# An MLP's two products on one core: residual by accumulating DMAs, gated fetches, two pairs stored late, weight loads in turn

## The chip, the cores and the metric

The kernel runs on one core of a Trainium2 chip. The metric is the device time of one execution in microseconds (us); of the kernel before it is the median of three runs, 2515.09 us (2513.76 to 2515.51). A core has TensorE (PE, with its weight loads as PEld), VectorE (DVE), ScalarE (ACT), GpSimd (POOL) and SyncE (SP). DMAs are issued here from SP and from POOL.

## The reference

One layer of a hybrid trunk on x of 512 x 2048 in float32: two branches (attention and a gated unit), merged and added to x, and then an MLP with a hidden width of 8192. The change touches the MLP alone:

```python
    x = x + merged @ w_out[l]
    h2 = rms_norm(x, g_ff[l])
    x = x + jnp.square(jax.nn.relu(h2 @ w_ff1[l])) @ w_ff2[l]
```

The `x` in front of the last `+` is called the residual below.

## The kernel before

**A product of float32.** Every operand is split into two parts, `hi` (cast on ACT, L107) and `lo` (the rest, by a subtraction on DVE, L108), and `mm3` (L70 to L74) issues three matmuls: hi x hi (L72), hi x lo (L73), lo x hi (L74). A weight thus goes from DRAM to a tile `w_raw`, through ACT to `w_hi`, through DVE to `w_lo`, and then to PE.

**Strassen's form.** Both MLP products use a scheme of seven products with sums of the four blocks of each operand. `NAMES` gives the seven names: y11, y21, m7, m6, y22, m4, m5. The class `Sums` (L161 to L190) loads the four weight blocks w11, w12, w21, w22 in its constructor (L169 and L170, each a DMA of 512 KB on SP), and makes the sums when a product is due: a = w11 + w21 on DVE for m7 (L176), an accumulating DMA on POOL that adds w22 to w21 (L178, where `loaded` is true; otherwise an addition on DVE for m5, L184), c = a + w22 for m6 (L180), c + w12 for y22 (L182). Six tiles per object: four blocks, a and c.

**The first product.** `hidden(p)` (L796) computes 256 hidden columns, a pair of 128, with `strassen_columns` (L192); there are 32 pairs, two of them computed plainly. The results of a pair (`act`, two tiles) are squared and made into the seven left operands of the second product, stored in DRAM as `store[f]`, f = p // 4. `keep_hidden` (L696) does it in steps that stand in the list `behind` and are called by `step()` while the following pair is computed. Pair 31, the last, goes through `keeping` (L732), seven steps of 256 KB each in chunk 1.

**The second product.** It goes over 8 chunks f of 1024 hidden columns, and in each over two halves g of 1024 output columns: `strassen_tokens` (L220). A half runs seven products; each has two row groups i, two token tiles t and two row blocks k, so 8 turns of `mm3` or 24 matmuls. Row group i = 0 takes its six weight tiles from the pool `raw`, i = 1 from the pool `more`, which is opened (L854) on the memory of the pool `long` when that is closed (L853). `long` holds twelve tiles that the first product reads: y11 of 8 blocks, and y21 of four (L686). The left operands come back from `store[f]` by `fetch(f, name)` (L813): four DMAs of 256 KB on POOL into tiles `ys` of the pool `slots`.

**The residual.** x after the branches lies in DRAM as `kept`. 16 tiles `x2` of 128 x 512 are loaded from it by `residual` (L837 to L840, 256 KB each on POOL), and `evac_y` (L866) adds each product's result to them on DVE (L869). In the last chunk the tiles go to the output.

**What orders the work.** The engines run their queues in order; a scheduler arranges the instructions by their dependences. `between(name)` (L875) is called behind each product and issues fetches; in chunk 0 it also issues residual loads. A DMA on SP or POOL waits, besides its data and its buffer, for the DMA eight places earlier on the same queue. `tc.issue_after` makes the instructions inside it depend on a given one. The last call of `hidden` and the first of `strassen_tokens` follow each other with no barrier.

Of the kernel before, what the change touches and what calls it, by code (L numbers as in the profile page):

```python
# [16 lines left out]
P = 128  # L17
# [18 lines left out]
def tile_hybrid_layer(ctx: ExitStack, tc: tile.TileContext, x, g_mix, w_in, g_q, g_k, ln_g, ln_b,  # L36
# [124 lines left out]
    class Sums:  # L161


        def __init__(self, blocks, tiles, loaded=True):


            self.blocks, self.loaded = blocks, loaded
            self.w11, self.w12, self.w21, self.w22, self.a, self.c = tiles
            for t, hc in ((self.w11, (0, 0)), (self.w12, (1, 0)), (self.w21, (0, 1)), (self.w22, (1, 1))):  # L169
                state["load"] = nc.sync.dma_start(out=t, in_=blocks[hc])  # L170
            self.take = {"y11": self.w11, "y21": self.w12, "m7": self.a, "m6": self.c, "y22": self.w12,
                         "m4": self.w22, "m5": self.w21}

        def parts(self, name):
# [17 lines left out]
    def strassen_columns(wap, c0, rhs, forks, evac, loaded=True):  # L192
# [4 lines left out]
        w = Sums(blocks, [state["raw"].tile([P, KH, P], F32, name="w_raw", tag="w_raw") for _ in range(6)],  # L197
                 loaded)
        trunk, side = acc("q"), acc("q")
        for name in TREE:  # L200
# [18 lines left out]

    def strassen_tokens(wap, r0, c0, lhs, evac, between, loaded=True, after=None):  # L220

        KQ = 2
        ws = []
        for i in range(2):
            rows = wap[r0 + i * 2 * KQ * P:r0 + (i + 1) * 2 * KQ * P, :]
            blocks = {(h, c): rows[:, c0 + c * W:c0 + (c + 1) * W].rearrange("(k h p) c -> h p k c", p=P, h=2)[h]
                      for h in range(2) for c in range(2)}
            pool = (state["raw"], state["more"])[i]
            ws.append(Sums(blocks, [pool.tile([P, KQ, W], F32, name="w_raw", tag="w_raw") for _ in range(6)],
                           loaded))  # L230
        banks = {}
        for name in NAMES:
            b, new = BANK[name]
            if new:
                banks[b] = [(aux if b in (1, 3) else acc)("q") for _ in range(2)]
            for i in range(2):
                with tc.issue_after(after.ins) if after and name == "m7" else nullcontext():
                    hi, lo = ws[i].parts(name)
                for t in range(2):
                    for k in range(KQ):  # L240
                        y = [part[:, t * P:(t + 1) * P] for part in lhs[name][i * KQ + k]]
                        mm3(banks[b][t], y, (hi[:, k, :], lo[:, k, :]), new and i == 0 and k == 0,
                            i == 1 and k == KQ - 1, skip_group_check=True)
            for t in range(2):
                evac(name, t, banks[b][t])
            between(name)
            step()
# [411 lines left out]

    def factor(ys, act, k, name, scale=None):  # L660


        y11, y12, y21, y22 = act[0][:, :HS], act[0][:, HS:], act[1][:, :HS], act[1][:, HS:]
        o, in0, in1, op = {"m7": (y22, y12, y22, ALU.subtract), "m6": (y22, y22, y11, ALU.subtract),
                           "m4": (y22, y21, y22, ALU.add), "m5": (y12, y11, y12, ALU.subtract)}[name]
        nc.vector.tensor_tensor(out=o, in0=in0, in1=in1, op=op)
        ys[name, k] = halves(o, scale=scale)

# [11 lines left out]
    for b in range(KT):  # L680
# [3 lines left out]
        for half in range(2):  # L684
            name = "y" + "12"[b % 2] + "12"[half]
            far = name == "y11" or name == "y21" and b // 2 < LONG - KT // 2  # L686
            hs[name, b // 2] = halves(y[:, half * HS:(half + 1) * HS], long if far else slots)
# [64 lines left out]
    for p in range(PLAIN):  # L752
        o = [acc("f1") for _ in range(2)]
        for kt in range(0, KT, 4):
            hi, lo = weight(w_ff1[0], kt, p * 2 * P, 2 * P)
            if p == PLAIN - 1:
                for i in range(kt, kt + 4):
                    factor(hs, x2T[i % 8 * 2:i % 8 * 2 + 2], i % 8, "m7" if i < 8 else "m6",
                           -1.0 if i < 8 else None)
            for c in range(2):  # L760
# [66 lines left out]
    pairs = DFF // (2 * P)  # L827
    for p in range(PLAIN, pairs - 1):
        acts.append(hidden(p))
# [3 lines left out]
        behind.extend([lambda fs=fs: [f() for f in fs if f] for fs in zip_longest(*ready)])  # L833
    act = hidden(pairs - 1)
    flush()

    def residual(half, t, c):  # L837
        tb, j = 2 * half + t, c
        x2[tb, j] = slot("x2")
        nc.gpsimd.dma_start(out=x2[tb, j], in_=kept[tb, j])  # L840

    lhs = {}

    def fetch_first(name):
        lhs[name] = fetch(0, name)
        if name in ("y11", "m7", "m6", "y22"):
            half, c = {"y11": (0, 0), "m7": (1, 1), "m6": (0, 1), "y22": (1, 0)}[name]
            for t in range(2):
                residual(half, t, c)

    for name in NAMES[:3]:
        fetch_first(name)
    first.close()  # L853
# [5 lines left out]
             "m5": [(1, 1, ALU.subtract), (1, 0, ALU.add)]}  # L859
    done = {"y21": [(0, 0)], "m4": [(0, 1)], "m5": [(1, 1), (1, 0)]}  # L860
    for f in range(chunks):
        ahead = {}
        if f == 1:
            behind.extend(keeping(pairs - 1, act))
        for g in range(2):
            def evac_y(name, t, o):  # L866
                for half, c, op in takes[name]:
                    a = x2[2 * half + t, 2 * g + c]
                    nc.vector.tensor_tensor(out=a, in0=a, in1=o, op=op)  # L869
                if f == chunks - 1:  # L870
                    for half, c in done.get(name, []):
                        tb, j = 2 * half + t, 2 * g + c
                        nc.sync.dma_start(out=out[tb * P:(tb + 1) * P, j * W:(j + 1) * W], in_=x2[tb, j])

            def between(name):  # L875
# [3 lines left out]
                if f == 0:  # L879
                    if g == 0 and i + 3 < len(NAMES):  # L880
                        fetch_first(NAMES[i + 3])
                    for half, c in {(0, "m4"): [(0, 2)], (1, "y11"): [(1, 3)], (1, "y21"): [(0, 3)],
                                    (1, "m7"): [(1, 2)]}.get((g, name), []):
                        for t in range(2):
                            residual(half, t, c)
                    i = i - 6 if g == 0 else i + 1
                    asked = 0 <= i < len(NAMES)
                else:
                    i += g * 5
                    asked = i < (5 if g == 0 else 7)  # L890
                if f < chunks - 1 and asked:
                    ahead[NAMES[i]] = fetch(f + 1, NAMES[i])

            strassen_tokens(w_ff2[0], f * GROUP * 2 * P, g * 2 * W, lhs, evac_y, between,
                            loaded=f > 0, after=None if f or g else state["evac"])
        lhs = ahead
# [25 lines left out]
```

## Time and profile before

| | |
|---|---|
| median of three runs | 2515.09 us |
| the profiled execution, its own time | 2515.18 us |
| its span in the profile | 2513.1 us |
| granted clock of PE, mean | 0.994 |
| PE busy | 2474.6 us (98%) |
| DVE busy | 1617.4 us (64%) |
| ACT busy | 1068.7 us (43%) |
| POOL busy | 329.4 us (13%) |
| DRAM traffic | 346.58 MB read, 67.11 MB written |

The time is the slowest core's whole execution; the span is from the first to the last recorded instruction, here 2.1 us less. Busy time is given by engine; the brackets behind an instruction give the idle time ahead of it and what ended it, so `[8.00 <-ACT w_hi L107]` is 8 us of waiting that ended with ACT's cast of line 107. `q` and `fork` are accumulators of PE, `ys` the left operands. The DMA share is the mean busy share of the 16 DMA engines. `SPq` and `POOLq` are the DMA queues of SP and POOL. The second product's first matmul starts at 1873.41 us in the span.

### The profile page before, as it was taken

What the parts mean: (1) busy time and instruction counts of PE and PEld (TensorE: products, weight loads), DVE (VectorE), ACT (ScalarE), POOL (GpSimd) and SP (SyncE); (2) the same over time, 40 slices, a digit from 0 to 9 for tenths busy, and PEclk for the clock granted to TensorE, in tenths of its full rate; (3) what the DMA queues carried; (4) which work ended last, traced back from release to release, by engine and by line L of the source; (5) the groups of instructions that cost most, each with busy time, mean ns of one, the idle gap of its engine ahead of it and who ended that gap; (6) DMA issues with size and microseconds to landing.
All of it is one profiled execution on the core that took longest, in us unless ns stands there. A gap on an engine that the chain in (4) does not pass through costs nothing.

```text
span 2513.1 us, 32248 instructions
## 1 busy us (share of the span) xinstructions
PE 2474.6 (98%) x12221; PEld 2092.2 (83%) x12221; DVE 1617.4 (64%) x2078; ACT 1068.7 (43%) x1507; POOL 329.4 (13%) x420
## 2 busy tenths in 40 slices
PE   8999999999999999999999999999988999999999
PEld 7888888888888888888888888888876888888887
DVE  4555463223335343322689888888878989889887
ACT  5233342122322322232467776777753443333333
POOL 0212110000121010100000000000023223212210
PEclk9999999999999999999999999999998999999999
DMA  5322222333333233344259888888887887767763
GB/s 176 92 84 76 92 68 92 94 100 97 114 100 101 93 100 118 118 149 136 85 141 266 217 225 230 221 230 234 216 293 288 260 280 243 229 219 215 250 180 96
DMA packets 346381, 415.82 MB, mean 165 GB/s; under 512 B 16961, under 2 KB 224369, under 8 KB 346225
## 3 DMA queue, kind: packets, MB, share of 16 engines
q1 hardware_dynamic: 289248, 320.94, 39.6%
q0 software_dynamic: 56976, 92.82, 15.5%
q8 instruction: 96, 1.57, 0.3%
q14 instruction: 61, 0.49, 0.1%
HBM read 346.58 MB, written 67.11 MB: 165 GB/s over the span
## 4 chain that ended last, share of the span: by engine, by line
PE 95%; DMA 2%; DVE 2%; ACT 1%; issue 0%; SPq 0%; POOL 0%; DVEq 0%; ACTq 0%; POOLq 0%
PE q L73 10%; PE q L72 10%; PE q L74 10%; PE q L209 7%; PE fork L209 7%; PE q L211 3%; PE fork L211 3%; PE xo L74 2%; PE xo L72 2%; PE xo L73 2%; PE gb L72 2%; PE gb L73 2%; PE gb L74 2%; PE ga L72 2%; PE ga L73 2%; PE ga L74 2%
## 5 line engine op out<-in xcount | busy, mean ns | idle before, releaser
L107 ACT CAST w_hi<-w_raw 128x1024 fp32r<-128x1024 f32 x434 | 456.8, 1052 | 558.6 <-PE q L73 357.0
L96 DVE TENSOR_TENSOR w_lo<-w_raw,w_hi 128x1024 fp32r<-128x1024 f32 x216 | 268.1, 1241 | 595.7 <-ACT w_hi L94 591.6
L108 DVE TENSOR_TENSOR w_lo<-w_raw,w_hi 128x1024 fp32r<-128x1024 f32 x434 | 530.7, 1224 | 142.9 <-ACT w_hi L107 142.1
L94 ACT CAST w_hi<-w_raw 128x1024 fp32r<-128x1024 f32 x216 | 227.2, 1052 | 664.7 <-PE ga L73 99.6
L73 PE MATMUL q<-w_lo,ys 128*128 128x512 f32 x896 | 351.8, 393 | 9.5 <-DVE w_lo L108 9.5
L74 PE MATMUL q<-w_hi,ys 128*128 128x512 f32 x896 | 350.8, 392 | 0.0
L72 PE MATMUL q<-w_hi,ys 128*128 128x512 f32 x896 | 316.8, 393 | 8.0 <-ACT w_hi L107 8.0
L209 PE MATMUL q<-ys,w_hi 128*128 128x512 f32 x720 | 260.9, 400 | 4.2 <-ACT fork L215 3.5
L209 PE MATMUL fork<-ys,w_hi 128*128 128x512 f32 x720 | 258.4, 399 | 0.3 <-ACT fork L215 0.3
L73 PEld LDWEIGHTS q<-w_lo,ys 128*128 128x128 f32 x896 | 169.6, 189 | 47.2 <-DVE w_lo L108 12.1
L72 PEld LDWEIGHTS q<-w_hi,ys 128*128 128x128 f32 x896 | 169.6, 189 | 43.9 <-ACT w_hi L107 8.4
L211 PE MATMUL q<-ys,w_lo 128*128 128x256 f32 x720 | 203.1, 282 | 0.0
L211 PE MATMUL fork<-ys,w_lo 128*128 128x256 f32 x720 | 202.5, 281 | 0.0
L74 PEld LDWEIGHTS q<-w_hi,ys 128*128 128x128 f32 x896 | 169.5, 189 | 35.2
L178 POOL DMA_DIRECT2D w_raw<-in_w_ff_dram x57 | 79.4, 1393 | 772.9 <-ACT relu L803 399.9
L869 DVE TENSOR_TENSOR x<-x,q 128x512 f32<-128x512 f32 x256 | 168.2, 683 | 5.7 <-PE q L74 4.1
L209 PEld LDWEIGHTS q<-ys,w_hi 128*128 128x128 f32 x720 | 136.2, 189 | 35.7 <-ACT fork L215 4.1
L209 PEld LDWEIGHTS fork<-ys,w_hi 128*128 128x128 f32 x720 | 135.5, 188 | 32.3 <-ACT fork L215 0.6
L818 POOL DMA_DIRECT2D ys<-store x224 | 124.6, 568 | 251.9 <-PE q L74 180.4
L211 PEld LDWEIGHTS q<-ys,w_lo 128*128 128x128 f32 x720 | 137.2, 190 | 1.2
L211 PEld LDWEIGHTS fork<-ys,w_lo 128*128 128x128 f32 x720 | 136.3, 189 | 1.2
L72 PE MATMUL xo<-w_hi,mT_hi 128*128 128x512 f32 x256 | 100.6, 393 | 0.0
(277 smaller groups left out, 4843.4 us busy)
## 6 DMA issues: line engine op xcount, KB each, us to landing
w_raw<-in_w_ff_dram SPq DMA_DIRECT2D x256, 512.0 KB, 5.4
w_raw<-in_w_in_dram SPq DMA_DIRECT2D x144, 512.0 KB, 3.5
ys<-store POOLq DMA_DIRECT2D x224, 256.0 KB, 6.0
w_raw<-in_w_ff_dram POOLq DMA_DIRECT2D x57, 512.0 KB, 6.8
store<-ys_hi SPq DMA_DIRECT2D x93, 256.0 KB, 4.8
store<-ys_lo SPq DMA_DIRECT2D x93, 256.0 KB, 5.5
w_raw<-in_w_out_dram SPq DMA_DIRECT2D x32, 512.0 KB, 3.7
store<-ys SPq DMA_DIRECT2D x38, 256.0 KB, 5.7
```

The costliest lines, as they stand in the source:

```text
L72: nc.tensor.matmul(o, lhsT=lh[0], rhs=rh[0], start=start, stop=False, **kw)
L73: nc.tensor.matmul(o, lhsT=lh[0], rhs=rh[1], start=False, stop=False, **kw)
L74: nc.tensor.matmul(o, lhsT=lh[1], rhs=rh[0], start=False, stop=stop, **kw)
L94: nc.scalar.copy(out=hi, in_=raw)
L96: nc.vector.tensor_tensor(out=lo, in0=raw, in1=f32(hi), op=ALU.subtract)
L107: nc.scalar.copy(out=hi, in_=src)
L108: state["lo"] = nc.vector.tensor_tensor(out=lo, in0=src, in1=f32(hi), op=ALU.subtract)
L178: nc.gpsimd.dma_start(out=self.w21, in_=self.blocks[1, 1], accum_op=ALU.add)
L209: nc.tensor.matmul(o, lhsT=hi[:, k, :], rhs=y, start=new, stop=False, skip_group_check=True)
L211: nc.tensor.matmul(o[:, :HS], lhsT=lo[:, k, :], rhs=y[:, :HS], start=False, stop=last, skip_group_check=True)
L818: nc.gpsimd.dma_start(out=f32(t), in_=store[f][HELD.index(name), p])
L869: nc.vector.tensor_tensor(out=a, in0=a, in1=o, op=op)
```

## The change

Six edits:

1. *Residual.* Tiles `total` take the place of `x2`. The first result that arrives in a tile is written by ACT with a scale of 1 or -1; all others are added by DVE as before. The residual comes in later: accumulating DMAs on POOL add `kept` to the totals, in chunk 2's second half and chunk 3's first, always to the half of the columns that is not computed then.
2. *Fetches of chunk 0 and 1.* Four names of chunk 0 are fetched at once, ahead of the second product. The other three, and all seven of chunk 1, are fetched one name per product, each behind a gate: a 4-wide multiplication on POOL that reads the total just evacuated.
3. *Pairs 30 and 31.* Both are stored by `keeping`, 14 steps in chunk 1; before, pair 30 was stored by `keep_hidden` during pair 31.
4. *Weight loads.* The constructor no longer loads; a generator `loads()` does, and `strassen_tokens` takes one load of each row group in turn.
5. *The pool `long`.* It holds m7 of four blocks in place of y21 of four blocks. m7 is the second product of `hidden`'s order (`TREE`), y21 the fourth.
6. *The last product* of the last half runs token tile by token tile.

```diff
-            for t, hc in ((self.w11, (0, 0)), (self.w12, (1, 0)), (self.w21, (0, 1)), (self.w22, (1, 1))):
-                state["load"] = nc.sync.dma_start(out=t, in_=blocks[hc])
+        def loads(self):
+            for t, hc in ((self.w11, (0, 0)), (self.w12, (1, 0)), (self.w21, (0, 1)), (self.w22, (1, 1))):
+                state["load"] = nc.sync.dma_start(out=t, in_=self.blocks[hc])
+                yield
...
+        collections.deque(zip(*[w.loads() for w in ws]), 0)
...
+            turns = [(i, t) for i in range(2) for t in range(2)]
+            if last and name == NAMES[-1]:
+                turns.sort(key=lambda it: it[1])
...
-            far = name == "y11" or name == "y21" and b // 2 < LONG - KT // 2
+            far = name == "y11"
...
-                           -1.0 if i < 8 else None)
+                           -1.0 if i < 8 else None, long if i < LONG - KT // 2 else slots)
...
-    for p in range(PLAIN, pairs - 1):
+    for p in range(PLAIN, pairs - 2):
...
-    for name in NAMES[:3]:
-        fetch_first(name)
+    kept_last = []
+    for p in range(pairs - 2, pairs):
+        kept_last.append((p, hidden(p)))
+        flush()
+
+    lhs = {name: fetch(0, name) for name in NAMES[:4]}
...
-            behind.extend(keeping(pairs - 1, act))
+            for p, act in reversed(kept_last):
+                behind.extend(keeping(p, act))
...
-                    a = x2[2 * half + t, 2 * g + c]
-                    nc.vector.tensor_tensor(out=a, in0=a, in1=o, op=op)
+                    key = 2 * half + t, 2 * g + c
+                    if key not in total:
+                        total[key] = slot("total")
+                        nc.scalar.activation(out=total[key], in_=o, func=AF.Copy,
+                                             scale=1.0 if op == ALU.add else -1.0)
+                    else:
+                        a = total[key]
+                        nc.vector.tensor_tensor(out=a, in0=a, in1=o, op=op)
...
+                    half, c, _ = takes[name][0]
+                    gate = nc.gpsimd.tensor_tensor(out=tiny(4, "gate"), in0=total[2 * half + 1, 2 * g + c][:, :4],
+                                                   in1=mhalf, op=ALU.mult)
+                    with tc.issue_after(gate.ins):
+                        if g == 0 and i + 4 < len(NAMES):
+                            lhs[NAMES[i + 4]] = fetch(0, NAMES[i + 4])
+                        if g == 1:
+                            ahead[name] = fetch(1, name)
+                    return
+                if (f, g) in ((2, 1), (3, 0)):
+                    for n in (i, len(NAMES)) if i == len(NAMES) - 1 else (i,):
+                        tb, j = n % NTB, 2 * (1 - g) + n // NTB
+                        nc.gpsimd.dma_start(out=total[tb, j], in_=kept[tb, j], accum_op=ALU.add)
```

The order of POOL's queue where the first product ends, before (`store_8736` is chunk 0, `store_8737` chunk 1, `x<-kept` a residual load):

```order
L818 DMA ys<-store_8736 128x512 x4
L840 DMA x_15690<-kept 128x512
L840 DMA x_15692<-kept 128x512
L818 DMA ys<-store_8736 128x512 x8
L840 DMA x_15710<-kept 128x512
L840 DMA x_15712<-kept 128x512
L818 DMA ys<-store_8736 128x512 x4
L840 DMA x_15782<-kept 128x512
```

And after, at the same place:

```order
L828 DMA ys<-store_8736 128x512 x16
L886 TENSOR_TENSOR gate<-total,mhalf 128x4
L828 DMA ys<-store_8736 128x512 x4
L886 TENSOR_TENSOR gate<-total,mhalf 128x4
L828 DMA ys<-store_8736 128x512 x4
L886 TENSOR_TENSOR gate<-total,mhalf 128x4
L828 DMA ys<-store_8736 128x512 x4
L886 TENSOR_TENSOR gate<-total,mhalf 128x4 x5
L828 DMA ys<-store_8737 128x512 x4
```

The residual loads are gone from it, 16 fetches stand together, and each further group of four stands behind a gate.

SP's queue at the same place, before (L705 and L713 are the stores of `keep_hidden`, L170 the weight loads; those with 128x2x512 belong to the second product):

```order
L170 DMA w_raw<-in_w_ff_dram 128x2x512
L705 DMA store_8743<-ys_lo 128x2x256
L170 DMA w_raw<-in_w_ff_dram 128x2x512 x2
L713 DMA store_8743<-ys 128x512
L705 DMA store_8743<-ys_hi 128x2x256
L705 DMA store_8743<-ys_lo 128x2x256
L170 DMA w_raw<-in_w_ff_dram 128x2x512 x4
L705 DMA store_8743<-ys_hi 128x2x256
L705 DMA store_8743<-ys_lo 128x2x256
L705 DMA store_8743<-ys_hi 128x2x256
L705 DMA store_8743<-ys_lo 128x2x256
L170 DMA w_raw<-in_w_ff_dram 128x2x512 x16
```

And after (L174 the weight loads, L715 the stores of `keep_hidden`, L755 those of `keeping`):

```order
L174 DMA w_raw<-in_w_ff_dram 128x2x512
L715 DMA store_8743<-ys_lo 128x2x256
L715 DMA store_8743<-ys_hi 128x2x256
L174 DMA w_raw<-in_w_ff_dram 128x2x512
L715 DMA store_8743<-ys_lo 128x2x256
L174 DMA w_raw<-in_w_ff_dram 128x2x512 x24
L755 DMA store_8743<-ys 128x512 x3
L174 DMA w_raw<-in_w_ff_dram 128x2x512 x8
```

The stores of pair 30 have left this place, and the loads stand together; the first eight of them are w11 and w12 of row group 0 (with stores among them), w11, w12, w21, w22 of row group 1, and w21 and w22 of row group 0.

More of the change, by code (lines that the diff above doesn't have):

```diff
@@ L198, in strassen_columns @@
                  loaded)
+        collections.deque(w.loads(), 0)
         trunk, side = acc("q"), acc("q")
@@ L218, in strassen_columns, with strassen_tokens @@
             step()
-    def strassen_tokens(wap, r0, c0, lhs, evac, between, loaded=True, after=None):
+    def strassen_tokens(wap, r0, c0, lhs, evac, between, loaded=True, after=None, last=False):
         KQ = 2
@@ L235, in strassen_tokens @@
                 banks[b] = [(aux if b in (1, 3) else acc)("q") for _ in range(2)]
[L236 to L243, printed above, removed]
+            factors = []
+            turns = [(i, t) for i in range(2) for t in range(2)]
+            if last and name == NAMES[-1]:
+                turns.sort(key=lambda it: it[1])
+            for i, t in turns:
+                if i == len(factors):
+                    with tc.issue_after(after.ins) if after and name == "m7" else nullcontext():
+                        factors.append(ws[i].parts(name))
+                hi, lo = factors[i]
+                for k in range(KQ):
+                    y = [part[:, t * P:(t + 1) * P] for part in lhs[name][i * KQ + k]]
+                    mm3(banks[b][t], y, (hi[:, k, :], lo[:, k, :]), new and i == 0 and k == 0,
+                        i == 1 and k == KQ - 1, skip_group_check=True)
             for t in range(2):
@@ L657, in tile_hybrid_layer, with factor @@
     along(rstd2, rstd_b)
-    def factor(ys, act, k, name, scale=None):
+    def factor(ys, act, k, name, scale=None, pool=slots):
         y11, y12, y21, y22 = act[0][:, :HS], act[0][:, HS:], act[1][:, :HS], act[1][:, HS:]
@@ L666, in factor @@
         nc.vector.tensor_tensor(out=o, in0=in0, in1=in1, op=op)
-        ys[name, k] = halves(o, scale=scale)
+        ys[name, k] = halves(o, pool, scale)
     def halves(src, pool=slots, scale=None):
@@ L833, in tile_hybrid_layer @@
         behind.extend([lambda fs=fs: [f() for f in fs if f] for fs in zip_longest(*ready)])
[L834 to L849, printed above, removed]
-    for name in NAMES[:3]:
-        fetch_first(name)
+    kept_last = []
[3 more added lines that the diff above has]
+    lhs = {name: fetch(0, name) for name in NAMES[:4]}
     first.close()
@@ L860, in tile_hybrid_layer @@
     done = {"y21": [(0, 0)], "m4": [(0, 1)], "m5": [(1, 1), (1, 0)]}
+    total = {}
     for f in range(chunks):
@@ L872, in evac_y @@
                         tb, j = 2 * half + t, 2 * g + c
-                        nc.sync.dma_start(out=out[tb * P:(tb + 1) * P, j * W:(j + 1) * W], in_=x2[tb, j])
+                        nc.sync.dma_start(out=out[tb * P:(tb + 1) * P, j * W:(j + 1) * W], in_=total[tb, j])
             def between(name):
@@ L879, in between @@
                 if f == 0:
[L880 to L891, printed above, removed]
+                    half, c, _ = takes[name][0]
[11 more added lines that the diff above has]
+                        nc.gpsimd.dma_start(out=total[tb, j], in_=kept[tb, j], accum_op=ALU.add)
+                i += g * 5
+                if f < chunks - 1 and i < (5 if g == 0 else 7):
                     ahead[NAMES[i]] = fetch(f + 1, NAMES[i])
             strassen_tokens(w_ff2[0], f * GROUP * 2 * P, g * 2 * W, lhs, evac_y, between,
-                            loaded=f > 0, after=None if f or g else state["evac"])
+                            loaded=f > 0, after=None if f or g else state["evac"],
+                            last=f == chunks - 1 and g == 1)
         lhs = ahead
```

## The prediction

> **What bounds the kernel now.** I read the page's first part, then one table of stretches, to see whether TensorE (PE) is the bound everywhere.
>
> ```profile
> span 2513.1 us, 32248 instructions
> PE 2474.6 (98%) x12221; PEld 2092.2 (83%) x12221; DVE 1617.4 (64%) x2078; ACT 1068.7 (43%) x1507; POOL 329.4 (13%) x420
> ```
>
> The table's columns are the stretch and its length, then busy time and instruction count of PE, PEld, DVE, ACT, POOL, then granted clock, DMA share, GB/s.
>
> ```profile
> 1.00:1870.00 1869.00, 1853.99 (x9514) 1581.25 (x9515) 1072.70 (x1482) 827.83 (x1271) 173.55 (x164) 1.00 0.50 143
> 1870.00:1945.00 75.00, 57.49 (x226) 44.83 (x225) 50.64 (x57) 22.08 (x26) 26.67 (x50) 0.89 0.83 312
> 1945.00:2500.00 555.00, 555.00 (x2451) 459.73 (x2450) 489.06 (x534) 217.84 (x212) 128.78 (x202) 1.00 0.72 222
> ```
>
> PE is the bound, and everything after 1945 runs without a gap: 555.00 of 555.00. Of the 38.5 us in which PE idles (2513.1 less 2474.6), 17.5 us lie in the 75 us where the first MLP product hands over to the second (75.00 less 57.49). So that is the stretch to price, by its matmuls. The second product starts here:
>
> ```profile
> 1873.41 0.40 PE L72 MATMUL q<-w_hi,ys 128*128 128x512 f32 x1
> 2507.70 0.39 PE L74 MATMUL q<-w_hi,ys 128*128 128x512 f32 x1
> ```
>
> It has 8 chunks x 2 halves x 7 products x 8 turns x 3 = 2688 matmuls (the code's loops). At the undisturbed pace, 555.00 / 2451 = 0.2264 us each, they need 608.7 us; from 1873.41 to the end of the last (2508.1) it takes 634.7. The loss is 26.0 us. The same from the stretch itself: 3.4 us of the first product, then 226 matmuls less some 19 of the first product = 207, x 0.2264 = 46.9; 75.0 less 50.3 is 24.7. The two differ because some records are missing from a trace. I take 25: 17.5 us of idle and some 7.5 us of matmuls at a lowered clock.
>
> What PE waits for, and what it runs at afterwards:
>
> ```profile
> 1884.30 0.80 PE L72 MATMUL q<-w_hi,ys 128*128 128x512 f32 x1 [8.00 <-ACT w_hi L107]
> 1898.78 0.80 PE L73 MATMUL q<-w_lo,ys 128*128 128x512 f32 x1 [4.96 <-DVE w_lo L108]
> ```
>
> ```profile
> 1883.20 1.04 ACT L107 CAST w_hi<-w_raw 128x1024 fp32r<-128x1024 f32 x1 [13.02 <-DMA w_raw<-in_w_ff_dram]
> ```
>
> ```profile
> 1882.00:1890.00 8.00, 5.24 (x12) 3.77 (x13) 4.58 (x6) 5.97 (x9) 4.21 (x8) 0.50 1.04 387
> 1898.00:1906.00 8.00, 7.22 (x20) 5.70 (x21) 7.76 (x9) 1.04 (x1) 5.00 (x10) 0.58 1.04 403
> 1906.00:1914.00 8.00, 8.00 (x37) 6.62 (x36) 4.39 (x5) 3.16 (x3) 4.14 (x8) 1.00 1.04 388
> ```
>
> PE names ACT and DVE, but ACT itself had waited 13.02 us for a weight load. Behind each wait the granted clock is 0.50 to 0.58 for 6 to 8 us, so a long wait costs almost half its length again.
>
> Why the loads are late is seen in the DMA part of the stretch 1850 to 1945 (count, size, median us to landing) and in the chain of waits:
>
> ```profile
> ys<-store POOLq DMA_DIRECT2D x51, 256.0 KB, 7.4
> w_raw<-in_w_ff_dram SPq DMA_DIRECT2D x18, 512.0 KB, 14.1
> x<-kept POOLq DMA_DIRECT2D x16, 256.0 KB, 7.2
> ```
>
> ```profile
> 1869.76 24.25 DMA w_raw<-in_w_ff_dram
> 1911.92 13.37 DMA w_raw<-in_w_ff_dram
> ```
>
> ```profile
> w_raw<-in_w_ff_dram SPq DMA_DIRECT2D x256, 512.0 KB, 5.4
> ```
>
> ```profile
> 1860.00:1880.00 20.00, 16.30 (x90) 13.70 (x88) 10.10 (x16) 7.92 (x13) 11.82 (x23) 1.00 1.04 400
> 1900.00:1920.00 20.00, 20.00 (x80) 16.28 (x79) 13.31 (x14) 6.31 (x6) 7.89 (x15) 0.88 1.04 391
> ```
>
> A weight load lands 5.4 us after its issue over the whole run, 14.1 us here, and up to 24.25 on the chain. The DMA engines are full (share 1.04, 390 to 400 GB/s): between 1854 and 1913, POOL puts out 44 fetches of the first two chunks and 16 residual loads, 60 x 256 KB = 15.7 MB, which alone takes 40 us at 391 GB/s, while the weights wait among them.
>
> **The change, part by part.** *What leaves the stretch.* The 16 residual loads (4.2 MB) become accumulating DMAs in chunks 2 and 3; seven stores of pair 30 (1.8 MB) go to chunk 1; chunk 1's 28 fetches (7.3 MB) no longer go out as soon as buffers are free but one name per product of the second half. At 391 GB/s these are 10.7 + 4.7 + 18.8 = 34 us of full DMA engines (estimates from that rate).
>
> *What moves ahead.* The rows of the order show four names fetched without a gate, in place of three mixed with residuals. The first fetch used to start here:
>
> ```profile
> 1854.02 1.69 POOL L818 DMA_DIRECT2D ys<-store  x3 [25.76 <-issue]
> 1834.00:1854.00 20.00, 20.00 (x124) 17.79 (x123) 16.85 (x24) 13.76 (x22) 0.00 (x0) 1.00 0.62 196
> ```
>
> The code now makes it wait for a buffer that DVE lets go some 20 us earlier (estimated from that instruction's place in DVE's order). 4.2 MB in those 20 us add 210 GB/s to 196: just what the engines carry. I expect them landed by about 1857.
>
> *The weight loads.* SP's rows of before:
>
> ```profile
> 1852.44 0.37 SPq L170 DMA_DIRECT2D w_raw<-in_w_ff_dram  x1
> 1864.11 8.35 SPq L170 DMA_DIRECT2D w_raw<-in_w_ff_dram  x4
> 1888.92 69.52 SPq L170 DMA_DIRECT2D w_raw<-in_w_ff_dram  x16
> ```
>
> The four loads of the second row group (i=1) left from 1864.11 to 1872.5, because the pool they go into came free only with the fourth product of the last pair. With m7's tiles in that place it comes free with the second, about 5.5 us earlier, near 1858; there they stand directly behind w11 and w12 of the first group. Eight loads, 4.2 MB, from 1852 on take 10.7 us at 391 GB/s: landed by 1865 to 1870. The first is needed at 1873.4, the second group's at 1873.4 + 12 x 0.2264 = 1876.1. Both waits of PE above go, I take 0 for them, and 8 us of low clock go with the idle.
>
> *What is late next.* The gates: the fetch of y22 waits for the first product's totals. That product ends at 1873.4 + 24 x 0.2264 = 1878.9. Then come two ACT copies and the gate on POOL, a 128x4 operation, near these rows:
>
> ```profile
> L215 ACT COPY fork<-q 128x512 f32<-128x512 f32 x87 | 50.7, 583 | 0.0
> L272 POOL TENSOR_TENSOR rstd<-ms,mhalf 128x4 f32<-128x4 f32 x1 | 1.0, 1022 | 178.6 <-DMA kept<-x 178.6
> ```
>
> 1878.9 + 1.2 + 1.0 = 1881; four issues of 0.54 with gaps of about 0.5 take 4, as in these rows,
>
> ```profile
> 1908.04 0.54 POOL L818 DMA_DIRECT2D ys<-store  x1 [0.56 <-DMA x<-kept]
> 1909.06 0.54 POOL L818 DMA_DIRECT2D ys<-store  x1 [0.48 <-DMA x<-kept]
> ```
>
> and the last lands 7.4 later even with full engines: 1892.5. y22 is the fifth product, due at 1873.4 + 4 x 5.43 = 1895.1. It fits with 2.6 us to spare, m4 and m5 likewise. Behind each gate on POOL only fetches are queued, since chunk 0 has no accumulation of weights. The second half of chunk 0, 38 us long, has 8 weight loads (4.2 MB) and 28 fetches (7.3 MB): 11.5 MB, 303 GB/s, below the 391 of the full stretch.
>
> *What a short wait costs.* Not every wait will go, so I price one. PE once waited 2.04 us in the first product, and its pairs of matmuls then came 0.64 us apart (1280.91, 1281.55), against 0.36 later (1284.52, 1284.87), up to 1283.3; a wait of 0.66 us left the clock at 1.00:
>
> ```profile
> 1280.11 0.79 PE L209 MATMUL q<-ys,w_hi 128*128 128x512 f32 x1 [2.04 <-ACT fork L215]
> 1280.91 0.63 PE L209 MATMUL q<-ys,w_hi 128*128 128x512 f32 x1
> 1281.55 0.63 PE L209 MATMUL q<-ys,w_hi 128*128 128x512 f32 x1
> 1284.52 0.40 PE L209 MATMUL fork<-ys,w_hi 128*128 128x512 f32 x1
> 1284.87 0.40 PE L209 MATMUL fork<-ys,w_hi 128*128 128x512 f32 x1
> 1280.00:1284.00 4.00, 3.89 (x13) 3.37 (x14) 3.19 (x3) 1.03 (x2) 0.00 (x0) 0.57 0.05 12
> 1293.00:1297.00 4.00, 3.09 (x16) 2.33 (x15) 3.20 (x8) 3.38 (x7) 0.00 (x0) 1.00 0.66 96
> ```
>
> 3.2 us at 0.36 / 0.64 of the pace lose 1.4 us, so a wait of 2 us costs 3.4, and one below 0.7 us itself. By the Trainium skill (TensorE: Matmul & The Clock Gate, Part 1: The HAM clock gate) the clock falls only after an idle window of about 3.4 us, and a wait of 2 us would cost 2. The row says otherwise, and the sum goes by the row; by the page a rest of one short wait would be 1.4 us less, 2490.6 in place of 2492.
>
> *Work that changes engines.* 16 of chunk 0's 32 additions on DVE become ACT copies of 0.58 us; ACT is idle over half the time there. DVE gains 16 x 0.68 us:
>
> ```profile
> L869 DVE TENSOR_TENSOR x<-x,q 128x512 f32<-128x512 f32 x256 | 168.2, 683 | 5.7 <-PE q L74 4.1
> ```
>
> On the path that is zero, as PE waits for loads and not for additions. The ACT copies can delay the cast behind them by 0.6 us; in PE's order m6's first matmuls stand inside m7, so I allow 0.6 us of stall.
>
> *Chunk 1.* It stores two pairs, in 14 steps over both halves, instead of one in 7. A step costs DVE a subtraction or two of 0.42 us:
>
> ```profile
> L108 DVE TENSOR_TENSOR ys<-relu,ys 128x256 fp32r<-128x256 f32 x38 | 15.9, 421 | 0.0
> L108 DVE TENSOR_TENSOR w_lo<-w_raw,w_hi 128x1024 fp32r<-128x1024 f32 x434 | 530.7, 1224 | 142.9 <-ACT w_hi L107 142.1
> ```
>
> From the rows, a half of 38.0 us (168 x 0.2264) has 20 operations of 1.22 and 16 of 0.68, 35.3 us; in a dense row they overlap by some 0.08, so about 33. Seven steps add 11 x 0.42 less overlap, about 3.7: under 37 of 38.0. Chunk 1's first half has carried just that without a gap in PE. The second half now does too: zero, with 2 us as upper bound.
>
> *The accumulations* in chunks 2 and 3 add 4.2 MB to 76 us at 222 GB/s (the stretch 1945 to 2500), 55 GB/s more, while POOL gains 16 issues. No accumulation into these tiles is in the trace: nearest row x<-kept, 7.2 us. The next addition on a tile comes 16 us or more later in the order, so zero; if an accumulation takes twice as long, still zero. *The last product's turns* let two of four additions run earlier, but two must still follow the last matmul: 0 to 0.3 us gained, I take 0.
>
> Sum against the profiled execution's 2515.2 us (0.1 above the median of 2515.09): 25 removed, 0.6 for m6's cast, and 1.4 for the low clock behind one short wait of a kind that may remain. 2515.2 - 25 + 2.0 = **2492 us**, rounded.
>
> **The rivals.** *The gates hold.* If fetches behind a gate land after 14.1 us as the weights did, instead of 7.4, y22 is 4 us late (14.1 - 7.4 - 2.6), PE stops once for it (m4 and m5 shift along) and then runs some 3 us at a lowered clock, another 1.4 to 2: about 2498. For it: a stream with several queues served last was slow in this stretch. Against: the 34 us of full DMA that leave. The same price, some 5 us, would come of DVE being overloaded in chunk 1, where a wait of 2 us costs 3.4 as well.
>
> *Half remains.* If the early fetches do not land by 1857, because their buffers come free later than their place in the order says, they meet the weights at 1852 to 1870 and the first wait of 8 us stays in part: 2498 to 2508, 2503 in the middle. Against: the fetches' share is 4.2 MB in place of 15.7.
>
> *The change doesn't free the path.* If w11 of the second group is late for the SP queue itself (stores of pair 29 ahead, each load waiting on the eighth before it), both waits stay whatever POOL does: 2510 to 2516, no change. SP's row of 8.35 us for four loads speaks for it; but those four waited for buffers.
>
> *Slower.* The accumulations stand on POOL's one queue, in chunks 2 and 3, where the fetches of the next chunk and the accumulation into w21 that m5 needs stand behind them. If an accumulation takes over twice a plain load (from 16 us on), DVE's additions wait for totals, banks stay full and PE stops, in both halves. Each stop of 12 us with 4 of low clock, twice, gives 2492 + 32 = 2524. Against: the DMA share there is 0.72, and POOL is 129 us busy of 555.
>
> **How the numbers follow.** The forecast, 2488 to 2496, has a chance of 0.64; the gates or DVE in chunk 1, to 2502, 0.17; half remaining, 2500 to 2508, 0.10; nothing freed 0.04; slower 0.05. About 0.2% (5 us) is what a measurement of this kernel can tell. From 2515.1, faster by that is below 2510.1: 0.91; same 0.04; slower 0.05. The low end is all of the 26 us gone and 1 us gained in the end, 2488; the high end, 2504, takes in the gates' case and half of "half remains", leaving out under 0.2.
>
> **What would show it.** Right: in 1870 to 1945 PE is busy for over 72 us, the clock is 0.97 or more, weight loads land within 8 us, DMA share falls below 0.9, and the first fetch is issued near 1834. Wrong: a wait of PE over 3 us behind y22's first matmul (gates), behind the second group's w11 near 1876 (half remains), in 1950 to 2025 (chunk 1), or additions of DVE that wait for an accumulation in chunks 3 and 4.

## The result and the profile after

The changed kernel takes 2491.99 us (median of 6 runs, 2491.06 to 2494.01) where the kernel before takes 2514.71 (6 runs, 2512.73 to 2515.51): a ratio of 0.9912, interval 0.9899 to 0.9925, 22.7 us less. The forecast was 2492.

First the page's head and the table of stretches of the kernel after (stretch, length, then busy time and count of PE, PEld, DVE, ACT, POOL, granted clock, DMA share, GB/s):

```profile
span 2490.5 us, 32273 instructions
PE 2467.4 (99%) x12221; PEld 2086.4 (84%) x12221; DVE 1606.4 (65%) x2065; ACT 1078.0 (43%) x1526; POOL 343.9 (14%) x434
```

```profile
1870.00:1945.00 75.00, 74.54 (x332) 61.50 (x331) 62.87 (x62) 40.35 (x50) 27.63 (x46) 1.00 0.70 236
1854.00:1874.00 20.00, 20.00 (x120) 17.68 (x119) 14.88 (x20) 13.71 (x22) 4.25 (x8) 1.00 0.96 348
1945.00:2021.00 76.00, 75.59 (x333) 62.03 (x332) 66.47 (x87) 32.62 (x40) 24.31 (x41) 1.00 0.91 306
2021.00:2098.00 77.00, 75.54 (x332) 61.91 (x332) 68.94 (x78) 30.11 (x30) 36.75 (x56) 1.00 1.01 304
2098.00:2175.00 77.00, 77.00 (x342) 63.71 (x341) 68.96 (x74) 29.56 (x28) 26.58 (x41) 1.00 0.90 265
```

The stretch from 1870 to 1945, which lost 17.5 us of idle and ran at a clock of 0.89, now loses 0.46 us and runs at 1.00. The DMA share in it falls from 0.83 to 0.70, and the full stretch lies ahead of it, at 1854 to 1874, where PE does not wait. New gaps are in the rows 1945 to 2021 and 2021 to 2098: 0.4 and 1.5 us, in three waits between 2015 and 2029, at the end of chunk 1 and just behind it. All the waits of PE from 1860 on (what it waited for, us in all, times, the longest):

```profile
PE q L73 <- DVE w_lo L108: 1.9, 3, 0.8
PE q L72 <- ACT w_hi L107: 0.5, 1, 0.5
```

The second product, from the start of its first matmul to the start of its last, falls from 634.3 us (1873.41 to 2507.70) to 612.9:

```profile
1872.21 0.40 PE L72 MATMUL q<-w_hi,ys 128*128 128x512 f32 x1
2485.06 0.39 PE L74 MATMUL q<-w_hi,ys 128*128 128x512 f32 x1
```

That is 21.4 of the 22.7 us. The rest is no part of it: over the fourteen profiles of this study the first matmul of the second product starts anywhere from 1870.84 to 1874.91, and in the changed kernel and two others that differ from it only from chunk 1 on it starts at 1872.21, 1874.29 and 1874.91. I therefore compare this length beside the times below; an undisturbed one is 2688 x 0.2264 = 608.6 us.

SP's weight loads and POOL's fetches where the products meet:

```profile
1852.21 0.37 SPq L174 DMA_DIRECT2D w_raw<-in_w_ff_dram  x1
1854.94 0.37 SPq L174 DMA_DIRECT2D w_raw<-in_w_ff_dram  x1
1856.83 92.31 SPq L174 DMA_DIRECT2D w_raw<-in_w_ff_dram  x24
```

```profile
1831.37 0.60 POOL L828 DMA_DIRECT2D ys<-store  x1 [4.30 <-ACT relu L813]
1855.53 2.77 POOL L828 DMA_DIRECT2D ys<-store  x5 [5.69 <-DVE relu L814]
1858.49 1.59 POOL L828 DMA_DIRECT2D ys<-store  x3 [0.19 <-DMA w_raw<-in_w_ff_dram]
1879.30 0.24 POOL L886 TENSOR_TENSOR gate<-total,mhalf 128x4 f32<-128x4 f32 x1 [19.22 <-ACT total L870]
1879.76 1.09 POOL L828 DMA_DIRECT2D ys<-store  x2 [0.22 <-issue]
1889.84 1.11 POOL L886 TENSOR_TENSOR gate<-total,mhalf 128x4 f32<-128x4 f32 x1 [7.45 <-DVE total L874]
1893.18 2.15 POOL L828 DMA_DIRECT2D ys<-store  x4
```

and the landing times of the DMAs issued from 1850 to 1945 (count, size, median us):

```profile
w_raw<-in_w_ff_dram SPq DMA_DIRECT2D x24, 512.0 KB, 8.5
ys<-store POOLq DMA_DIRECT2D x40, 256.0 KB, 6.8
```

The loads of the second row group leave from 1856.83 on in place of 1864.11. The 8.5 us are a median over the loads of three halves, most of them issued later. The loads that this product needs first, those issued from 1856.8 to 1863.9, landed more slowly; the second line is the second row group's four in the kernel before (1863.9 to 1875):

```profile
w_raw<-in_w_ff_dram SPq DMA_DIRECT2D x6, 512.0 KB, 11.6
w_raw<-in_w_ff_dram SPq DMA_DIRECT2D x4, 512.0 KB, 24.1
```

So the loads still crowd each other, but they come in time. The closest of those whose landing the trace tells is w21 of the first row group, the seventh of the eight: it landed at 1872.7, and DVE's two sums for m7, the first to need it, begin some 2 us later with no wait for a DMA:

```profile
1874.85 2.35 DVE L179 TENSOR_TENSOR w_raw<-w_raw 128x1024 f32<-128x1024 f32 x2
```

### The profile page after: what moved, and what is told of

Read it like the earlier page. It is cut to its first block, busy times and chain, and to the rows that moved or that the text cites. A ratio compares the mean times of both kernels' runs of the same rounds, so it can differ in the third digit from the quotient of the medians.

```text
span 2490.5 us, 32273 instructions
## 1 busy us (share of the span) xinstructions
PE 2467.4 (99%) x12221; PEld 2086.4 (84%) x12221; DVE 1606.4 (65%) x2065; ACT 1078.0 (43%) x1526; POOL 343.9 (14%) x434
## 4 chain that ended last, share of the span: by engine, by line
PE 96%; DVE 2%; issue 1%; DMA 1%; ACT 1%; POOL 0%; SPq 0%; DVEq 0%; POOLq 0%; ACTq 0%
PE q L72 10%; PE q L73 10%; PE q L74 10%; PE fork L213 7%; PE q L213 7%; PE fork L215 3%; PE q L215 3%; PE xo L74 2%; PE xo L72 2%; PE xo L73 2%; PE gb L72 2%; PE gb L74 2%; PE gb L73 2%; PE ga L72 2%; PE ga L73 2%; PE ga L74 2%
## 5 line engine op out<-in xcount | busy, mean ns | idle before, releaser
L74 PE MATMUL q<-w_hi,ys 128*128 128x512 f32 x896 | 348.7, 389 | 0.0
L72 PE MATMUL q<-w_hi,ys 128*128 128x512 f32 x896 | 312.0, 389 | 0.5 <-ACT w_hi L107 0.5
L874 DVE TENSOR_TENSOR total<-total,q 128x512 f32<-128x512 f32 x240 | 157.2, 682 | 5.9 <-PE q L74 4.5
```

The costliest lines, as they stand in the source:

```text
L72: nc.tensor.matmul(o, lhsT=lh[0], rhs=rh[0], start=start, stop=False, **kw)
L74: nc.tensor.matmul(o, lhsT=lh[1], rhs=rh[0], start=False, stop=stop, **kw)
```

## The experiments

Theory 1 (bytes): transfers that nobody needed yet kept the DMA engines full, and the weights landed late among them. Theory 2 (buffers): the second row group's loads were issued late, for want of their pool. Each kernel ran beside the kernel before on the same chip, but not all on one chip: the medians of the kernel before differ by up to 1.2 us, and the changed kernel was timed only for the result. "Length" is the second product's, first matmul to last, in the profile. Edit 6 and the fourth name fetched ahead were not run alone.

| kernel | median us | before, same chip | length us |
|---|---|---|---|
| before | 2514.71 | | 634.3 |
| after | 2491.99 | 2514.71 | 612.9 |
| after, edit 1 undone | 2498.62 | 2513.66 | 618.7 |
| after, no gates | 2495.80 | 2513.66 | 616.1 |
| after, edits 4 and 5 undone | 2491.62 | 2513.66 | 612.5 |
| after, edit 3 undone | 2495.31 | 2513.66 | 615.5 |
| after, 16 thick DMAs more | 2495.50 | 2514.06 | 615.1 |
| after, 16 thin DMAs more | 2491.46 | 2514.06 | 612.1 |
| before, edits 4 and 5 alone | 2515.62 | 2514.06 | 634.9 |
| before, edit 1 alone | 2506.27 | 2514.06 | 627.4 |
| before, edit 3 alone | 2504.91 | 2514.83 | 624.6 |
| before, edits 1 and 3 | 2498.16 | 2514.83 | 617.6 |
| after, accumulations twice | 2498.56 | 2514.83 | 615.5 |
| after, pair 30 in chunk 3 | 2491.67 | 2514.83 | 610.3 |

### The residual undone

```diff
-    lhs = {name: fetch(0, name) for name in NAMES[:4]}
...
+    for name in NAMES[:4]:
+        lhs[name] = fetch(0, name)
+        half, c = {"y11": (0, 0), "y21": (1, 1), "m7": (0, 1), "m6": (1, 0)}[name]
+        for t in range(2):
+            residual(half, t, c)
...
```

> The changed kernel (2492 us) with its first edit undone: the 16 residual loads of 256 KB stand on POOL again, eight with the first four names and eight with chunk 0's later products, and DVE does every addition. Theory 1 (bytes): the loss of the kernel before was DMA engines kept full by transfers that nobody needed yet; 4.2 MB more are 10.7 us of full engines at 391 GB/s, half of it ahead of the second product, so a wait of 2 to 5 us with its low clock returns: 2495 to 2500. Theory 2 (buffers): the loss was that the second row group's weight loads were issued late, for want of their pool; those loads still leave near 1857, so 2492 to 2494.

2498.62 us (2496.90 to 2499.81), 6.6 more than the changed kernel: theory 1, at the upper part of its range. In this kernel DVE's sum for m7, which needs w11 and w21, waits for the load of w21, and PE waits for DVE:

```profile
1880.71 2.36 DVE L179 TENSOR_TENSOR w_raw<-w_raw 128x1024 f32<-128x1024 f32 x2 [4.02 <-DMA w_raw<-in_w_ff_dram]
```

```profile
1884.26 0.50 PE L73 MATMUL q<-w_lo,ys 128*128 128x512 f32 x1 [1.68 <-DVE w_lo L108]
1891.13 0.50 PE L73 MATMUL q<-w_lo,ys 128*128 128x512 f32 x1 [3.62 <-DVE w_lo L108]
```

In the changed kernel the same two sums start at 1874.85, with no wait for a DMA. So the weight that is late next is not the second group's first but w21, which both groups need for the third product; by its landing, at 1880.7, it is the first group's.

### The gates taken out

```diff
...
-                    with tc.issue_after(gate.ins):
-                        if g == 0 and i + 4 < len(NAMES):
-                            lhs[NAMES[i + 4]] = fetch(0, NAMES[i + 4])
-                        if g == 1:
-                            ahead[name] = fetch(1, name)
+                    if g == 0 and i + 4 < len(NAMES):
+                        lhs[NAMES[i + 4]] = fetch(0, NAMES[i + 4])
+                    i = i - 6 if g == 0 else i + 1
+                    if 0 <= i < len(NAMES):
+                        ahead[NAMES[i]] = fetch(1, NAMES[i])
```

> The changed kernel with the gates taken out: chunk 0's last three names and chunk 1's seven are fetched as soon as buffers are free, as before. Theory 1 (bytes): up to 7.3 MB, 18.8 us of full engines, come back among the weight loads of chunk 0's second half, which are issued late; PE waits there for some 4 to 8 us: 2497 to 2503. Theory 2 (buffers): the eight loads of the first half are issued before these fetches, so 2492 to 2494.

2495.80 us (2495.07 to 2496.12), 3.8 more: theory 1 by its sign, 1.2 us below its range. The place is not the one expected, chunk 0's second half, but the sums for m7 in the first half again:

```profile
1880.81 2.36 DVE L179 TENSOR_TENSOR w_raw<-w_raw 128x1024 f32<-128x1024 f32 x2 [5.75 <-DMA w_raw<-in_w_ff_dram]
```

```profile
1884.37 0.78 PE L73 MATMUL q<-w_lo,ys 128*128 128x512 f32 x1 [3.19 <-DVE w_lo L108]
```

### Edits 4 and 5 undone

```diff
-            far = name == "y11"
+            far = name == "y11" or name == "y21" and b // 2 < LONG - KT // 2
...
-        collections.deque(zip(*[w.loads() for w in ws]), 0)
+        for w in ws:
+            collections.deque(w.loads(), 0)
...
```

> The changed kernel with edits 4 and 5 undone: y21's tiles are in the pool that row group 1's weights wait for, and the loads go group by group. Residual, gates and late stores stay. Theory 1 (bytes): the loads leave at 1864 to 1866 on engines that are not full, land within 8 us, by 1874, before 1876 when they are needed: 2492 to 2495. Theory 2 (buffers): the first wait of 8 us returns with its low clock: 2500 to 2508.

2491.62 us (2490.60 to 2494.62): no difference from the changed kernel. The second group's loads do leave late again, from 1861.13 on:

```profile
1861.13 0.88 SPq L174 DMA_DIRECT2D w_raw<-in_w_ff_dram  x2
```

That is 9.7 us ahead of this kernel's first matmul of the second product (1870.84), as in the kernel before (9.3), against 15.4 in the changed kernel; but the first of them lands after 7.5 us, at 1868.6. Theory 2 falls as a need: with the other transfers gone, the earlier leaving is worth nothing that these runs can tell. This run shared its chip with the three others that undo an edit, so their 6.6, 3.8 and 3.3 us do not come of the chip.

### Pair 30 stored as before

```diff
-    for p in range(PLAIN, pairs - 2):
+    for p in range(PLAIN, pairs - 1):
...
-    for p in range(pairs - 2, pairs):
+    for p in range(pairs - 1, pairs):
```

> The changed kernel with edit 3 undone: pair 30 is stored during pair 31 again (seven stores of 256 KB among SP's weight loads), and chunk 1 has seven steps in place of 14. Theory 1 (bytes): 1.8 MB, 4.7 us of full engines, and SP issues them between the loads, so the second group's loads leave and land some 3 us later than 1870, just in time: 2492 to 2496, less the 1.9 us of short waits in chunk 1 that the 14 steps brought. Theory 2 (buffers): no wait comes back, 2490 to 2492.

2495.31 us (2494.58 to 2495.94), 3.3 more, in theory 1's range. The sums for m7 wait for w21 here too, and PE for the lo part made of them:

```profile
1879.10 2.36 DVE L179 TENSOR_TENSOR w_raw<-w_raw 128x1024 f32<-128x1024 f32 x2 [3.04 <-DMA w_raw<-in_w_ff_dram]
```

```profile
1886.06 0.79 PE L73 MATMUL q<-w_lo,ys 128*128 128x512 f32 x1 [3.97 <-DVE w_lo L108]
```

This run also shows which edit lets the fetches go early. Its first one:

```profile
1854.01 1.68 POOL L828 DMA_DIRECT2D ys<-store  x3 [25.85 <-issue]
```

That is where the kernel before had it (1854.02), against 1831.37 in the changed kernel. By the code, pair 30's factors, when they are made during pair 31, stand ahead of the fetches in the pool of tiles; that this is the reason follows from the code alone.

### Sixteen DMAs more, thick and thin

```diff
+    spare = dram.tile([NTB, 4, P, W], F32, name="spare")
...
+        with tc.issue_after(state["fetched"].ins):
+            nc.gpsimd.dma_start(out=spare[tb, j][:, :512], in_=kept[tb, j][:, :512])
```

(`:4` in place of `:512` for the thin ones.) They go from DRAM to DRAM, and both kinds stand on POOL's queue where the residual loads stood in the first experiment.

> The changed kernel with 16 further DMAs of 256 KB on POOL, from DRAM to a spare DRAM buffer that nothing reads, at the places where the residual loads stood in the run with the first edit undone (2498.6 us there): eight among the first four names, eight behind the gates. No tile and no addition depends on them. Theory 1 (bytes): the 4.2 MB alone cost what the residual loads cost, 2496 to 2502, with w21 of the second product landing near 1880 instead of before 1875. Theory 3 (buffers and DVE): what cost time there was the tiles that the residual holds and the additions that DVE took back from ACT; then this runs at 2492 to 2494.

> As the run before, at the same places of POOL's queue, but each of the 16 DMAs moves 128 x 4 elements (2 KB) in place of 256 KB. Theory 1 (bytes): 32 KB are nothing, 2491 to 2493. Theory 4 (queue): what counts is the place on POOL's queue, where each DMA takes 0.54 us to issue and waits for the one eight places earlier; then it costs as much as the thick ones, 2496 or more.

Thick 2495.50 us (2494.07 to 2497.18), thin 2491.46 (2490.36 to 2493.53). The bytes alone cost 4.0 us against the thin ones on the same chip (3.5 against the changed kernel), half a us below theory 1's range; the places on the queue cost nothing. This is theory 1 measured by itself. In the thick run the sums for m7 wait for w21 again,

```profile
1877.54 2.36 DVE L179 TENSOR_TENSOR w_raw<-w_raw 128x1024 f32<-128x1024 f32 x2 [1.17 <-DMA w_raw<-in_w_ff_dram]
```

```profile
1886.77 0.50 PE L73 MATMUL q<-w_lo,ys 128*128 128x512 f32 x1 [1.56 <-DVE w_lo L108]
```

and the waits at the end of chunk 1 grow from 1.9 to 2.9 us. The cost is over half of the 6.6 us of the residual undone: the rest goes with the tiles and DVE's additions, and these runs don't part the two.

### The earlier weight loads alone

```diff
-            for t, hc in ((self.w11, (0, 0)), (self.w12, (1, 0)), (self.w21, (0, 1)), (self.w22, (1, 1))):
-                state["load"] = nc.sync.dma_start(out=t, in_=blocks[hc])
...
+        collections.deque(zip(*[w.loads() for w in ws]), 0)
...
-            far = name == "y11" or name == "y21" and b // 2 < LONG - KT // 2
+            far = name == "y11"
...
```

> The kernel before with edits 4 and 5 alone: weight loads in turn, m7's tiles in the pool long, so that the second group's loads leave some 6 us earlier. Residual loads, ungated fetches and pair 30's stores stay. Theory 1 (bytes): the engines stay full, the loads land 14 us and more after they leave; a few us gained at the first wait, 2508 to 2513. Theory 2 (buffers), which the run with both edits undone has already spoken against as a need: the first wait of 8 us goes with its low clock, 2498 to 2503.

2515.62 us (2513.90 to 2517.83), ratio 1.0004 (0.9995 to 1.0014): nothing gained, not even the few us of theory 1. The loads do leave earlier, in this kernel

```profile
1858.25 4.69 SPq L174 DMA_DIRECT2D w_raw<-in_w_ff_dram  x6
```

but each takes longer to land than the one before it, up to 18.7 us by the trace, and those of the next half, which leave from 1883.22 on, take 21.6. So the waits change places: 8.0 and 5.0 us became 5.75 and 15.56. First the loads issued from 1856.8 to 1863.9 and those from 1875 to 1900, then the two waits:

```profile
w_raw<-in_w_ff_dram SPq DMA_DIRECT2D x6, 512.0 KB, 13.1
w_raw<-in_w_ff_dram SPq DMA_DIRECT2D x6, 512.0 KB, 21.6
```

```profile
1887.94 0.80 PE L73 MATMUL q<-w_lo,ys 128*128 128x512 f32 x1 [5.75 <-DVE w_lo L108]
1927.23 0.80 PE L73 MATMUL q<-w_lo,ys 128*128 128x512 f32 x1 [15.56 <-DVE w_lo L108]
```

### Edits 1 and 3, alone and together

The edits are those of the diff, put into the kernel before.

> The kernel before with edit 1 alone: the residual by accumulating DMAs in chunks 2 and 3, first totals by ACT. Theory 1 (bytes): 4.2 of some 20 MB leave, but the 44 fetches follow one another faster and fill the engines until about 1905; the gain is 4 to 9 us, 2505 to 2510. Theory 2 (buffers): the second group's loads still leave at 1864 and later, no gain, 2512 to 2514.

> The kernel before with edit 3 alone: pairs 30 and 31 both stored in chunk 1. Theory 1 (bytes): 1.8 MB leave the stretch, and the first fetches go out some 20 us earlier, as no tile of pair 30's factors is in their place; 16 residual loads and 28 fetches of chunk 1 stay and keep the engines full to about 1905. Gain 5 to 10 us: 2504 to 2509. If pair 30's stores were only the 4.7 us of engine time that their bytes take: 2510 to 2512.

> The kernel before with edits 1 and 3, without gates and without the earlier weight loads. Theory 1 (bytes): 6 MB leave; what remains is the changed kernel without gates but for edits 4 and 5, which did nothing where they were alone or undone: 2494 to 2498, beside 2495.8 of the run without gates. If edits 4 and 5 matter once the engines are no longer full: 2499 to 2504.

Edit 1 alone 2506.27 us (7.8 less than the kernel before on the same chip), edit 3 alone 2504.91 (9.9 less), both 2498.16 (16.7 less). All three lie in or at theory 1's ranges. Together they give nearly their sum. Which of the two is worth more isn't shown, as the intervals of their ratios overlap (0.9957 to 0.9981, and 0.9947 to 0.9977). That edit 3 gains 9.9 us, though it takes away 1.8 MB and not 4.2, speaks against counting bytes alone: it also sends the first fetches out 20 us earlier, as the run with it undone showed. Edits 4 and 5 without gates may be worth something (2498.16 here, 2495.80 without gates only): the two ran on different chips, their ratios' intervals overlap, and the kernels differ in the fourth name fetched ahead as well, so the time leaves this open. In the profile of edits 1 and 3 PE still waits for the second group's first weight, which it doesn't without gates:

```profile
1877.78 0.49 PE L72 MATMUL q<-w_hi,ys 128*128 128x512 f32 x1 [1.51 <-ACT w_hi L107]
```

### Accumulations twice

```diff
-                        nc.gpsimd.dma_start(out=total[tb, j], in_=kept[tb, j], accum_op=ALU.add)
+                        for _ in range(2):
+                            nc.gpsimd.dma_start(out=total[tb, j], in_=kept[tb, j], accum_op=ALU.add)
```

> The changed kernel with each of the 16 accumulating DMAs issued twice, so that the residual is added twice. 4.2 MB more on POOL's queue in chunks 2 and 3, each second DMA waiting for the first on the same tile. If the accumulations have the slack that the prediction gave them (the next addition on a tile comes 16 us or more later): 2491 to 2494. If they are near the point from which DVE waits for a total: 2500 or more, with DVE's additions waiting for a DMA.

2498.56 us (2496.17 to 2499.64), 6.6 more than the changed kernel, of which the profiled length shows 2.6; where the rest lies isn't shown. Neither reading was right: there is a cost, but no addition waits for a total. What DVE waits for in chunks 2 and 3 of this kernel (2040 to 2175), longest line first but for ACT's casts, is weights again, 7.9 us against 1.7 in the changed kernel (the last two lines):

```profile
DVE w_raw L179 <- DMA w_raw<-in_w_ff_dram: 5.1, 3, 2.1
DVE w_raw L183 <- DMA w_raw<-in_w_ff_dram: 2.8, 3, 1.8
DVE w_raw L179 <- DMA w_raw<-in_w_ff_dram: 0.9, 1, 0.9
DVE w_raw L183 <- DMA w_raw<-in_w_ff_dram: 0.8, 1, 0.8
```

```profile
2098.00:2175.00 77.00, 74.85 (x328) 61.04 (x327) 65.33 (x71) 28.47 (x27) 36.28 (x53) 1.00 1.07 315
```

The DMA share is 1.07 where the changed kernel has 0.90: the engines are full, as they were between the products before.

### Pair 30 in chunk 3

```diff
-            for p, act in reversed(kept_last):
-                behind.extend(keeping(p, act))
+            behind.extend(keeping(*kept_last[1]))
+        if f == 3:
+            behind.extend(keeping(*kept_last[0]))
```

> The changed kernel with pair 31 stored in chunk 1 and pair 30 in chunk 3, seven steps each, in place of 14 steps in chunk 1. If chunk 1's waits of PE for DVE (0.4 and 1.5 us) come of the 14 steps on DVE, they go, and with them any low clock behind them: 1.5 to 3 us less, 2489 to 2491. If they come of the fetches or the weight loads there, no change.

2491.67 us (2490.89 to 2493.32), ratio 0.9911 (0.9894 to 0.9927): no difference in time. In the profile the waits at the end of chunk 1 are gone, PE being busy all through chunk 1 and most of chunk 2,

```profile
1945.00:2021.00 76.00, 76.00 (x337) 62.94 (x336) 68.88 (x83) 32.00 (x35) 29.75 (x52) 1.00 0.93 312
2021.00:2098.00 77.00, 77.00 (x342) 63.75 (x341) 67.30 (x75) 30.26 (x30) 30.81 (x44) 1.00 0.95 277
```

and the length is 2.5 us shorter, 610.3. So the waits did come of the 14 steps. A gain of 2 us isn't shown by the times: it is less than the start of the second product varies.

## Why the prediction was right, and where its steps were not

**The loss that goes (25 us).** Right: 21.4 us of it went, between the same two matmuls. The cause, full DMA engines, is shown by the thick and thin DMAs, and by the three edits that each bring back a wait for w21 when undone. That the median falls on the forecast's 2492 within 0.1 us is luck: in the two profiles 1.2 us of the gain are the earlier start of the product, which varies by more than that.

**The weight loads' earlier leaving.** Wrong as a cause. The prediction let both waits go partly because the second group's loads leave 5.5 us earlier; they do (by 6.1, counted from the product's start), but undoing it costs nothing, and doing it alone gains nothing. Of its signs this one failed: the loads there land after 9.3 to 12.3 us by the trace, not within 8, and w21 at 1872.7, not by 1870. The margin was some 2 us, and each of the three undone edits uses it up.

**The early fetches ("landed by about 1857").** Mis-sized. The first leaves at 1831, earlier than the 1834 given, but POOL then waits for buffers and the last eight go out from 1855.5 to 1860, among the weight loads (DMA share 0.96 at 1854 to 1874). The last lands at 1868.5 by the trace, where the prediction had 1857. So the condition of the rival "half remains" came true and its price didn't: no wait came back, as only half of the sixteen fetches met the weights. Nor did I see that edit 3 is what sets them free; I put its worth at 1.8 MB of traffic, and alone it is 9.9 us.

**The gates.** The first opens at 1879.3, 1881 in the working, which starts the product 1.2 us later. Of m4 and m5 I wrote "likewise", and that failed: the second gate waited 7.45 us for an addition of DVE, so their fetches left between 1890.9 and 1895.3. By the trace m4's four landed at 1895.8, 1897.3, 1898.7 and 1899.5. PE puts m4's first matmuls inside y22: the first that waits for m4's first fetch starts at 1896.36, the one for its third at 1899.08, 0.6 and 0.4 us behind the landings. PE did not wait, but with almost nothing to spare. That rival was nearer than its reasons made it.

**m6's cast.** The size was right, 0.6 allowed and 0.46 us measured, of this very cast; the reason isn't borne out. The cast stands behind no ACT copy: ACT is idle for 1.66 us before it, until a matmul of PE releases it.

```profile
1883.08 1.05 ACT L107 CAST w_hi<-w_raw 128x1024 fp32r<-128x1024 f32 x1 [1.66 <-PE q L73]
```

**The rest of 1.4 us, and chunk 1.** The sum held by exchange. The low clock of one short wait did not come; in its place came the 1.9 us of DVE's lateness at the end of chunk 1, which I had put at zero with 2 us as the bound. The run with pair 30 in chunk 3 shows its cause.

**The accumulations.** Zero was right for the kernel as it is, and for the reason given: no addition waits for a total. But the slack is not the 16 us until the next addition; it is the DMA engines, whose share in 2021 to 2098 is already 1.01 (0.81 in the kernel before). Pricing the accumulations by their bytes undersized them, as the last section shows. The rival on the slower side named the wrong thing to run out.

**The last product's turns.** 0 was right: DVE's four last additions and the tail behind the last matmul are as before, 5.4 us each time (2507.70 to 2513.1, 2485.06 to 2490.5).

## What to carry to other kernels

A wait that names a cast or a sum is followed to the load behind it, and a load that lands late while the DMA share is at 1 is cured by taking other transfers out of that stretch, not by issuing it sooner: issued sooner among the same traffic, it only moved the wait. Where several things crowd a stretch, each edit undone alone understates its worth (6.6, 3.8 and 3.3 us here, of 22.7), so take them also alone, in the kernel before. And count a store that moves away not only by its bytes: the tiles that it held may be what the fetches behind it wait for.

## What the runs showed of the hardware

The clock falls behind some waits of 2 to 4 us and not behind others of the same length. In the run with edit 3 alone, a wait of 2.39 us was followed by a clock of 0.50 and one of 2.96 us by 1.00:

```profile
1877.22 0.80 PE L72 MATMUL q<-w_hi,ys 128*128 128x512 f32 x1 [2.39 <-ACT w_hi L107]
1919.02 0.50 PE L73 MATMUL q<-w_lo,ys 128*128 128x512 f32 x1 [2.96 <-DVE w_lo L108]
```

The traces show why. In all fourteen, up to the tail behind the last matmul, a stretch of clock 0.50 lasts 3.41, 6.83, 10.24 or 17.07 us, whole steps of 3.41, and within a trace all of them begin on one grid of such steps. Where the clock was full, every step with 1.9 us or more of idle in PE was followed by a low one, and none with less than 1.86 (from 20 us on). The wait of 2.39 us put 2.13 us into one step; the longer one was cut by the end of a step into 1.87 and 1.10. The rows are steps of that grid, each wait's first and the one that follows it:

```profile
1873.55:1876.96 3.41, 1.28 (x6) 0.74 (x4) 0.00 (x0) 0.83 (x1) 1.61 (x3) 1.00 1.03 381
1876.96:1880.37 3.41, 2.68 (x6) 1.81 (x7) 3.13 (x5) 2.79 (x6) 1.19 (x3) 0.50 1.04 390
1914.51:1917.92 3.41, 1.55 (x7) 0.94 (x5) 3.41 (x5) 1.05 (x1) 0.00 (x0) 1.00 0.02 8
1917.92:1921.33 3.41, 2.31 (x10) 1.94 (x11) 3.41 (x4) 0.00 (x0) 0.00 (x0) 1.00 0.00 0
```

So the prediction's 3.4 us for a wait of 2 us hold only where nearly all of it falls into one step; elsewhere the wait costs its own length. The Trainium skill (TensorE: Matmul & The Clock Gate, Part 1: The HAM clock gate) says that the window over which activity is judged runs freely; the grid agrees.

With accumulating DMAs among them the engines are full at a lower rate: 304 GB/s at a share of 1.01 (2021 to 2098 of the changed kernel), where the plain transfers between the products of the kernel before reached 391 at 1.04. The packets of the trace fit that: in that stretch one of 2 KB takes 194 ns on average in the accumulating DMAs and 91 ns in the weight loads.
